# Second-layer MLP: the sums of the first weight's quarters for Strassen's products, moved from GpSimd to DVE

## The chip, the cores and the metric

The kernel runs on one core of one Trainium2 chip, in one launch. The metric is device time in microseconds (us), the median of several runs; the profiled execution is a run of its own with its own time. Engines are called as the profile calls them: PE (TensorE matmul), PEld (its weight load), DVE (VectorE), ACT (ScalarE), POOL (GpSimd), SP (SyncE, which here only issues DMAs).

## What is computed

Two layers of a diffusion backbone over 512 latent tokens, with 256 context tokens that only the first layer carries on. Layer 0 mixes by pooling, layer 1 by grouped-query attention; each ends in an MLP with a squared ReLU. Model width 1024, MLP width 4096, all in float32.

```
def sq_relu_mlp(h, w1, w2):
    return jnp.square(jax.nn.relu(h @ w1)) @ w2
...
    for i in range(DEPTH):
...
        h_lat = h_lat + g1[:, None, :] * y_l
        m_l = modulate(rms_norm(h_lat, norm_g[i, 1]), sh2, sc2)
        h_lat = h_lat + g2[:, None, :] * sq_relu_mlp(m_l, mlp_w1[i], mlp_w2[i])
        if ctx_out:
            h_ctx = h_ctx + cg1[:, None, :] * y_c
            m_c = modulate(rms_norm(h_ctx, norm_g[i, 1]), csh2, csc2)
            h_ctx = h_ctx + cg2[:, None, :] * sq_relu_mlp(m_c, mlp_w1[i], mlp_w2[i])
    return rms_norm(h_lat, final_g)
```

`ctx_out` holds in the first layer only, so the second layer's MLP has the 512 latent tokens alone.

## The kernel before

Every float32 operand of a matmul is split into a high part (float32r, written by ACT, line 86) and a low part (the rest, written by a subtraction on DVE, line 87; `hilo`), and a product is made as high by high, high by low, low by high: three matmuls into one PSUM tile.

`mlp` takes the MLP width in 16 chunks of 256. In chunk c it makes the hidden activations `act` (the first weight, m1), and then the second weight's products of the chunk before (`m2_chunk`, line 490): eight PSUM tiles, each of six matmuls of 512 columns, each added into the residual `h_lat` by one DVE instruction (line 348, called an eviction below). In the second layer chunks 0 to 3 make m1 plainly (line 371; ReLU, two squares on ACT, lines 379 to 382, and the low part on DVE, line 383). Chunks 4 to 15 use Strassen's scheme (`m1_strassen`): seven products of 48 matmuls over halves of both operands in place of eight. For it, each pair of weight tiles is loaded by two DMAs (line 510) into a tile `fin` of two buffers, and five of the seven weight operands are sums or differences of two quarters of it (line 428, into the scratch tile `sc`, 128x512). ACT and DVE then split each operand into high and low parts (lines 433 and 434 for the two that are negated, 86 and 87 for the others). The matmuls (line 439) go to one tile of the PSUM pool `mm` (two buffers) and two of `aux` (four buffers); lines 444 to 450 add the products up, lines 464 to 467 make the activations. The sums on the side of the tokens are made once per layer by DVE (`strassen_inputs`, lines 396, 397 and 87, into `xs`, or in place in `m_m_hi` and `m_m_lo`), beside the first chunks.

At the head of the MLP the normed tokens are made in steps (`modulated`: line 315 on DVE multiplies by the norm, lines 319 on ACT and 321 on DVE scale and shift, then the two parts go to `m_m_hi` and `m_m_lo`); the first chunk's matmuls follow these steps for the second half of the tokens.

Except where an order is written out by hand (the first layer's head), a scheduler of the framework puts each engine's instructions into one queue from priorities, dependences and buffers. Each engine runs its queue strictly in order, so an instruction that waits holds up all that stand behind it. The sums and the low part of the seventh operand were all in POOL's queue, where nothing else stood between them.

`m1_strassen` is used by both layers: the first calls it with `m` set (it needs the context tokens too), the second without.

Of the kernel before, what the change touches and what calls it, by code (L numbers as in the profile page):

```python
# [47 lines left out]
def dit_block_kernel(ctx: ExitStack, tc: tile.TileContext, xT, cols, adab, adaw, w1, w2, wqkv, wo,  # L48
                     poolw, gvec, rope, edge, eye, out):
    nc = tc.nc  # L50
    act, dve, pool, pe = nc.scalar, nc.vector, nc.gpsimd, nc.tensor
# [22 lines left out]
    def new(p, shape, dt, tag, bufs=None):  # L74
        uid[0] += 1
        kw = {"bufs": bufs} if bufs else {}
        return p.tile(shape, dt, tag=tag, name=f"{tag}{uid[0]}", **kw)

    def ps_mm():
        return new(mm, [P, 1024], F32, "mm")  # L80

    def ps_aux():
        return new(aux, [P, 512], F32, "aux")

    def hilo(hi, lo, src, lo_eng=dve):
        act.activation(hi, src, AF.Copy)  # L86
        lo_eng.tensor_tensor(lo, src, hi.bitcast(F32), op=ALU.subtract)  # L87
# [158 lines left out]
    def new_m(name, ctx_too=True):  # L246

        parts = [[big.tile([P, KT, SEQ], F32R, tag=t, name=f"{name}_{t}") for t in ("m_hi", "m_lo")]]
        if ctx_too:
            parts.append([[mc.tile([P, 4, CTX], F32R, tag="mc", name=f"{name}_c{x}{i}") for i in range(2)] for x in range(2)])  # L250
        return parts

    def ms(m, x, k, c0, n):
        if c0 < SEQ:
            return m[0][x][:, k, c0 : c0 + n]
        k0, k = (k.start // 4, slice(k.start % 4, (k.stop - 1) % 4 + 1)) if isinstance(k, slice) else (k // 4, k % 4)
        return m[1][x][k0][:, k, c0 - SEQ : c0 - SEQ + n]
# [153 lines left out]
    def m1_strassen(raw, inputs, a, op, m=None):  # L411


        op = op()
        a11, a12, a21, a22 = (raw[:, i, 512 * j : 512 * j + 512] for i in range(2) for j in range(2))
        ps, px, py = ps_mm(), ps_aux(), ps_aux()
        places = [ps[:, i * 256 : i * 256 + 256] for i in range(4)] + [px[:, :256], px[:, 256:], py[:, :256]]
        parts = [(a11, a12, ALU.add, -1), (a11, None, None, 1), (a22, None, None, 1), (a21, a22, ALU.add, -1),
                 (a12, a22, ALU.subtract, 1), (a21, a11, ALU.subtract, 1), (a11, a22, ALU.add, 1)]
        if m:  # L420
            parts += [(a12, None, None, 1), (a21, None, None, 1)]
        got = []
        for n, (x, y, how, sign) in enumerate(parts):
            w = op(n)
            got.append(w)
            if y is not None:
                t = new(sc, [P, 512], F32, "sc")
                pool.tensor_tensor(t, x, y, op=how)  # L428
                x = t
            if sign > 0:  # L430
                hilo(w[:, 0], w[:, 1], x, pool if n == 6 else dve)
            else:
                act.activation(w[:, 0], x, AF.Copy, scale=-1.0)
                dve.scalar_tensor_tensor(w[:, 1], x, -1.0, w[:, 0].bitcast(F32), op0=ALU.mult, op1=ALU.subtract)
            if n < 7:
                for k in range(4):
                    for wx in range(2):
                        for ax in range(2 - wx):
                            pe.matmul(places[n], w[:, wx, k * P : k * P + P], inputs[n][ax][:, k],  # L439
                                      start=k + wx + ax == 0, stop=k == 3 and wx == 1)  # L440

        q = ps.rearrange("p (q n) -> p q n", q=4)
        t = new(sc, [P, 2, 256], F32, "sc")
        act.activation(t, q[:, 0::3], AF.Copy)
        c, d = (new(rp, [P, T], F32, "r")[:, :512].rearrange("p (q n) -> p q n", q=2) for _ in range(2))
        dve.tensor_tensor(c, q[:, 1:3], t, op=ALU.subtract)
        for i in range(2):
            dve.tensor_tensor(d[:, i], q[:, 2 - i], t[:, i], op=ALU.add)  # L448
        dve.tensor_tensor(d, d, px.rearrange("p (q n) -> p q n", q=2), op=ALU.add)
        dve.tensor_tensor(d, d, py[:, :256].unsqueeze(1).to_broadcast([P, 2, 256]), op=ALU.add)  # L450
        blocks = a.rearrange("p t x (b n) -> p (t x b) n", n=256)
        todo = [(c, c, 1, 5), (d, d, 0, 7)]
        if m:
            pc = ps_aux()
            for t, ws in enumerate(((got[1], got[7]), (got[8], got[2]))):
                for k in range(KT):
                    for wx in range(2):
                        for ax in range(2 - wx):
                            pe.matmul(pc[:, t * 256 : t * 256 + 256], ws[k // 4][:, wx, k % 4 * P : k % 4 * P + P],  # L459
                                      ms(m, ax, k, SEQ, CTX), start=k + wx + ax == 0, stop=k == KT - 1 and wx == 1)  # L460
            todo.append((new(sc, [P, 2, 256], F32, "sc"), pc.rearrange("p (q n) -> p q n", q=2), 2, 6))
        for r, src, o, stride in todo:
            hi, lo = (blocks[:, o + x : o + x + stride + 1 : stride] for x in (0, 3))
            act.activation(r, src, AF.Relu)
            act.activation(hi, r, AF.Square)
            act.activation(r, r, AF.Square)  # L466
            dve.tensor_tensor(lo, r, hi.bitcast(F32), op=ALU.subtract)  # L467
# [29 lines left out]
    def mlp(i, m, total, last, first=None, between=None, ahead=None, strassen=None, acts=(), ws=()):  # L497
        gate = mod[i][:, 40:48]
        prev, acts, sides = None, list(acts), []
        for c in range(NCH):  # L500
# [3 lines left out]
            if not acts:  # L504
                several = 2 if first and c == 0 else 1
                acts = [new(ap_, [P, 2, 2, T], F32R, "act") for _ in range(several)]
                if strassen and c > 1 and c >= strassen[0]:
                    raw = strassen[2]()
                    for t in range(2):
                        nc.sync.dma_start(raw[:, t], w1[i, 2 * c + t])  # L510
                    m1_strassen(raw, inputs, acts[0], strassen[3], m if total > SEQ else None)
                    ws = ()
                else:
                    ws = ws or [load_w(w1[i, 2 * c + t]) for t in range(2 * several)]
                outs = [a[:, t] for a in acts for t in range(2)]
                if not ws:
                    pass
                elif several > 1:
                    m1_chunk(ws, outs, m, first)
                else:  # L520
                    for t in range(2):
                        m1_chunk(ws[t : t + 1], outs[t : t + 1], m, [[(0, total)]])
                ws = ()
# [76 lines left out]
    for s, c0, n in segs:  # L600
        rr = rstd_cols(n, [accs[s]], ps_aux())
        for i in range(n // P):
            t = turned[s][:, i]
# [87 lines left out]
    m = new_m("m")  # L691
# [488 lines left out]
```

## Time and profile before

| what | value |
|---|---|
| median of 3 runs | 1278.03 us (1275.25 to 1279.51) |
| the profiled execution: its own time | 1278.06 us |
| its span, first to last instruction | 1275.9 us (2.2 us lie around it) |
| mean granted clock of PE | 0.993 |
| busy: PE / DVE / ACT / POOL | 1238.5 / 1020.1 / 585.7 / 261.4 us |
| POOL, line 428 on `fin` (second layer) | 60 sums, 96.3 us |
| POOL, line 428 on `pair` (first layer) | 55 sums, 76.6 us |

The span's last 350 us are the second layer's MLP. Times in the timeline are from the span's start. A timeline row gives the start, the time from there to the end of the last of its instructions, engine, line, operation, tiles, and in brackets how long the engine had been idle before it and what ended that. Instructions of one engine overlap a little: the distance between two starts (the pitch) is shorter than the duration of one.

### The profile page before, as it was taken

Reading aid. Unit: us, or ns where it says so; the run is one execution under the profiler, and the core shown is the slowest. Engines: PE = TensorE matmul, PEld = TensorE weight load, DVE = VectorE, ACT = ScalarE, POOL = GpSimd, SP = SyncE. Lnnn points to the kernel's source line nnn. Section 1 sums busy time; section 2 is a strip of 40 time slices with the busy share of each in tenths; the row PEclk is TensorE's granted clock in tenths of the full one; section 3 lists DMA queues with packets and bytes.
Section 4 is the critical chain, followed back from the end, with each engine's and each line's share of the span. In section 5 each row is a group of like instructions: output and inputs, shape, how many; then the busy total and the mean of one; then the engine's idle time right before and its main releaser. Section 6 shows DMA issues by size and latency. Waiting matters only on the chain. (4 is left out here: it accounts for less than half of the span.)

```text
span 1275.9 us, 20565 instructions
## 1 busy us (share of the span) xinstructions
PE 1238.5 (97%) x8150; PEld 1102.5 (86%) x8150; DVE 1020.1 (80%) x1680; ACT 585.7 (46%) x1052; POOL 261.4 (20%) x200
## 2 busy tenths in 40 slices
PE   7999999999999999999999999999989999999997
PEld 6567888899999999999888899899978898989896
DVE  6564998778989888866888378879899889898976
ACT  6445523444444444433455254446554454544443
POOL 0000000122121322231012121211031334343412
PEclk8999999999999999999999999999999999999998
DMA  9666424333433333311113011111223322322111
GB/s 353 263 266 215 135 78 152 116 116 116 148 114 134 118 132 119 118 63 33 56 69 100 20 52 32 65 34 66 100 67 107 125 100 99 100 100 100 67 34 67
DMA packets 41313, 138.68 MB, mean 109 GB/s; under 512 B 4737, under 2 KB 8065, under 8 KB 41089
## 3 DMA queue, kind: packets, MB, share of 16 engines
q1 hardware_dynamic: 41216, 137.36, 30.9%
q8 instruction: 64, 1.05, 0.4%
q14 instruction: 33, 0.26, 0.1%
HBM read 135.25 MB, written 2.10 MB: 108 GB/s over the span
## 5 line engine op out<-in xcount | busy, mean ns | idle before, releaser
L490 PE MATMUL mm<-act,w 128*128 128x512 f32 (+1 forms) x1224 | 237.9, 345 | 3.9 <-DVE act L383 2.1
L490 PE MATMUL aux<-act,w 128*128 128x512 f32 (+1 forms) x1224 | 238.7, 346 | 0.3 <-DVE h_lat L348 0.2
L490 PEld LDWEIGHTS mm<-act,w 128*128 128x128 f32 x1224 | 195.1, 189 | 35.3 <-DVE act L383 2.4
L490 PEld LDWEIGHTS aux<-act,w 128*128 128x128 f32 x1224 | 194.8, 189 | 29.5 <-DVE h_lat L348 0.7
L86 ACT ACTIVATE w<-raw 128x1024 fp32r<-128x1024 f32 x106 | 110.1, 1055 | 124.5 <-PE aux L490 90.0
L428 POOL TENSOR_TENSOR sc<-pair 128x512 f32<-128x512 f32 x55 | 76.6, 1400 | 321.1 <-DVE h_lat L348 107.2
L87 DVE TENSOR_TENSOR w<-raw,w 128x1024 fp32r<-128x1024 f32 x96 | 116.9, 1232 | 28.4 <-ACT w L86 27.9
L348 DVE SCALAR_TENSOR_TENSOR h_lat<-aux,mod,h_lat 128x512 f32<-128x512 f32 (+1 forms) x204 | 125.6, 630 | 16.1 <-PE aux L490 14.7
L428 POOL TENSOR_TENSOR sc<-fin 128x512 f32<-128x512 f32 x60 | 96.3, 1620 | 172.7 <-DVE r L448 83.5
L348 DVE SCALAR_TENSOR_TENSOR h_lat<-mm,mod,h_lat 128x512 f32<-128x512 f32 (+1 forms) x140 | 96.6, 699 | 5.5 <-PE mm L490 4.0
L371 PE MATMUL mm<-m_m_hi,w 128*128 128x512 f32 (+1 forms) x320 | 92.5, 351 | 1.1 <-ACT m_m_hi L86 1.1
L860 PE MATMUL aux<-w,a_m_hi 128*128 128x256 f32 (+1 forms) x384 | 86.3, 320 | 0.0
L219 DVE SCALAR_TENSOR_TENSOR mc<-raw,s_f,mc 128x512 f32<-128x512 f32 x112 | 83.5, 766 | 1.9 <-DMA raw<-in_dram 1.1
L439 PE MATMUL mm<-m_m_hi,mc 128*128 128x256 f32 x384 | 71.0, 283 | 0.0
L860 PEld LDWEIGHTS aux<-w,a_m_hi 128*128 128x128 f32 x384 | 63.4, 190 | 5.0
L371 PEld LDWEIGHTS mm<-m_m_hi,w 128*128 128x128 f32 x320 | 56.1, 189 | 11.0 <-ACT m_m_hi L86 1.3
L459 PE MATMUL aux<-m_c,w 128*128 128x256 f32 x528 | 65.2, 283 | 0.0
L459 PEld LDWEIGHTS aux<-m_c,w 128*128 128x128 f32 x528 | 64.2, 192 | 0.0
L467 DVE TENSOR_TENSOR act<-r,act 128x512 fp32r<-128x512 f32 x46 | 48.4, 1052 | 19.6 <-ACT r L466 19.5
L860 PE MATMUL aux<-w,a_m_lo 128*128 128x256 f32 (+1 forms) x192 | 61.2, 319 | 0.0
L439 PEld LDWEIGHTS mm<-m_m_hi,mc 128*128 128x128 f32 x384 | 60.7, 192 | 0.5
L371 PE MATMUL mm<-m_m_lo,w 128*128 128x512 f32 (+1 forms) x160 | 56.3, 352 | 1.6 <-DVE m_m_lo L87 1.6
(245 smaller groups left out, 2530.5 us busy)
## 6 DMA issues: line engine op xcount, KB each, us to landing
raw<-in_dram SPq DMA_DIRECT2D x157, 512.0 KB, 3.3
praw<-in_dram SPq DMA_DIRECT2D x34, 512.0 KB, 8.2
fin<-in_dram SPq DMA_DIRECT2D x24, 512.0 KB, 4.1
pair<-in_dram SPq DMA_DIRECT2D x22, 512.0 KB, 4.3
block<-in_dram SPq DMA_DIRECT2D x8, 512.0 KB, 6.2
h_lat<-in_dram SPq DMA_DIRECT2D x4, 512.0 KB, 5.9
w<-in_dram SPq DMA_DIRECT2D x4, 512.0 KB, 10.7
out_dram<-fin SPq DMA_DIRECT2D x8, 256.0 KB, 2.5
```

The costliest lines, as they stand in the source:

```text
L86: act.activation(hi, src, AF.Copy)
L87: lo_eng.tensor_tensor(lo, src, hi.bitcast(F32), op=ALU.subtract)
L219: dve.scalar_tensor_tensor(acc[:, s], w, scal, acc[:, s], op0=ALU.mult, op1=ALU.add)
L348: dve.scalar_tensor_tensor(h, ps, gate[:, dt, s : s + 1], h, op0=ALU.mult, op1=ALU.add)
L371: pe.matmul(ps[:, c0 : c0 + cn], lhs, ms(m, ax, k, c0, cn), start=k + wx + ax == 0, stop=k == KT - 1 and wx == 1)
L428: pool.tensor_tensor(t, x, y, op=how)
L439: pe.matmul(places[n], w[:, wx, k * P : k * P + P], inputs[n][ax][:, k], start=k + wx + ax == 0, stop=k == 3 and wx == 1)
L459: pe.matmul(pc[:, t * 256 : t * 256 + 256], ws[k // 4][:, wx, k % 4 * P : k % 4 * P + P], ms(m, ax, k, SEQ, CTX), start=k + wx + ax == 0, ...
L467: dve.tensor_tensor(lo, r, hi.bitcast(F32), op=ALU.subtract)
L490: pe.matmul(ps, lhs, a[:, t, ax, c0 : c0 + n], start=t + wx + ax == 0, stop=t == 1 and wx == 1)
L860: pe.matmul(ps, lhs, ws[u][:, wx, o : o + width], start=k + ax + wx == 0, stop=k == KT - 1 and ax == 1)
```

## The change

In the second layer the engine of the five sums, and of the low part of the seventh operand, becomes DVE; in the first layer both stay on POOL.

```
     def m1_strassen(raw, inputs, a, op, m=None):
-        op = op()
+        op, eng = op(), pool if m else dve
...
             if y is not None:
                 t = new(sc, [P, 512], F32, "sc")
-                pool.tensor_tensor(t, x, y, op=how)
+                eng.tensor_tensor(t, x, y, op=how)
                 x = t
             if sign > 0:
-                hilo(w[:, 0], w[:, 1], x, pool if n == 6 else dve)
+                hilo(w[:, 0], w[:, 1], x, eng if n == 6 else dve)
```

So 60 sums and 12 subtractions, 72 instructions of 128x512, leave POOL's queue and stand in DVE's. The queues of PE and ACT change only in order, from the head of the second layer's MLP on; the DMA queue has one load moved by one place. Three places of DVE's queue follow, each as the difference (+ is the changed kernel).

First the head of the MLP, last quarter of the normed tokens (`sc_9629` is its scratch tile, `sc_9623` that of the quarter before; `fin_10284` is the first weight pair for Strassen; `mc_9894` and `mc_9895` are token sums):

```order
 L315 TENSOR_TENSOR sc_9629<-h_lat,mc_9609 128x512
+L428 TENSOR_TENSOR sc_10292<-fin_10284 128x512
+L87 TENSOR_TENSOR m_m_lo<-sc_9623,m_m_hi 128x2x256
 L321 TENSOR_SCALAR sc_9629<-sc_9629,am_140,mod_135 128x256
-L87 TENSOR_TENSOR m_m_lo<-sc_9623,m_m_hi 128x2x256
+L428 TENSOR_TENSOR sc_10339<-fin_10284 128x512
+L428 TENSOR_TENSOR sc_10356<-fin_10284 128x512
 L87 TENSOR_TENSOR m_m_lo<-sc_9629,m_m_hi 128x2x256
 L396 TENSOR_TENSOR mc_9894<-m_m_hi 128x1024
+L428 TENSOR_TENSOR sc_10372<-fin_10284 128x512
 L396 TENSOR_TENSOR mc_9895<-m_m_lo 128x1024
 L87 TENSOR_TENSOR w_9884<-raw_9885,w_9884 128x1024
```

Three sums now stand ahead of the last quarter's low part, and a fourth between the two token sums behind it.

Then the rows right behind these, up to the low part of the first activations (`act_9645`, line 383), which the first m2 block needs:

```order
 L87 TENSOR_TENSOR h_ctx_10287<-sc_10372,h_ctx_10287 128x512
 L397 TENSOR_TENSOR mc_9894<-mc_9894,mc_9895 128x1024
-L396 TENSOR_TENSOR mc_10046<-m_m_hi 128x1024
-L396 TENSOR_TENSOR mc_10047<-m_m_lo 128x1024
+L428 TENSOR_TENSOR sc_10388<-fin_10284 128x512
 L383 TENSOR_TENSOR act_9645<-r_9861,act_9645 128x512
 L383 TENSOR_TENSOR act_9645<-r_9866,act_9645 128x512
```

Two token sums of 1024 columns went behind the activations, and the fifth weight sum came ahead of them.

Last a chunk in the run of equal ones (`sc_11833`, `sc_11850`, `sc_11866` are sums for the next chunk; `mm_11703` and the like are m2 tiles being evicted):

```order
 L348 SCALAR_TENSOR_TENSOR h_lat<-mm_11703,mod_135,h_lat 128x512
-L434 SCALAR_TENSOR_TENSOR mc_11832<-sc_11833,mc_11832 128x512
+L428 TENSOR_TENSOR sc_11833<-fin_11778 128x512
 L348 SCALAR_TENSOR_TENSOR h_lat<-mm_11711,mod_135,h_lat 128x512
 L467 TENSOR_TENSOR act_11565<-r_11689,act_11565 128x2x256
 L348 SCALAR_TENSOR_TENSOR h_lat<-aux_11719,mod_135,h_lat 128x512
+L434 SCALAR_TENSOR_TENSOR mc_11832<-sc_11833,mc_11832 128x512
+L428 TENSOR_TENSOR sc_11850<-fin_11778 128x512
+L348 SCALAR_TENSOR_TENSOR h_lat<-aux_11727,mod_135,h_lat 128x512
+L428 TENSOR_TENSOR sc_11866<-fin_11778 128x512
+L348 SCALAR_TENSOR_TENSOR h_lat<-mm_11735,mod_135,h_lat 128x512
```

Sums and evictions now alternate, with at most two other instructions between two evictions, and at least two rows between a sum and the instruction that splits it.

## Rows read from the trace of the kernel before

**Rows 1.** Stretches: length, busy time of engines (instructions), PE's clock, DMA share, GB/s.
```profile
925.00:945.00 20.00, 15.25 (x119) 14.32 (x118) 19.12 (x20) 11.27 (x19) 8.53 (x5) 1.00 0.08 27
945.00:966.50 21.50, 21.50 (x94) 17.37 (x94) 21.15 (x24) 11.37 (x16) 1.99 (x1) 1.00 0.41 128
...
1009.92:1030.90 20.98, 20.98 (x133) 19.08 (x133) 18.01 (x25) 9.82 (x18) 8.84 (x7) 1.00 0.29 102
...
1177.76:1198.74 20.98, 20.98 (x133) 19.09 (x133) 18.01 (x25) 9.82 (x18) 8.85 (x7) 1.00 0.29 101
```

**Rows 2.** Timeline of PE at the head of the second layer's MLP.
```profile
930.02 0.50 PE L371 MATMUL mm<-m_m_hi,w 128*128 128x256 f32 x2 [1.05 <-ACT m_m_hi L86]
...
932.02 0.39 PE L371 MATMUL mm<-m_m_lo,w 128*128 128x256 f32 x1 [0.79 <-DVE m_m_lo L87]
...
933.93 0.39 PE L371 MATMUL mm<-m_m_lo,w 128*128 128x256 f32 x1 [0.81 <-DVE m_m_lo L87]
...
942.31 0.39 PE L490 MATMUL mm<-act,w 128*128 128x512 f32 x1
944.80 1.20 PE L490 MATMUL mm<-act,w 128*128 128x512 f32 x4 [2.10 <-DVE act L383]
```

**Rows 3.** Chain that ended last, in order of time: start, length, what.
```profile
956.15 10.88 PE mm L371 x48
...
1020.83 5.75 PE mm L439 x48
```

**Rows 4.** Timeline of DVE at the head of the second layer's MLP.
```profile
927.86 1.38 DVE L321 TENSOR_SCALAR sc<-sc,am,mod 128x256 f32<-128x256 f32 x1
929.16 1.75 DVE L315 TENSOR_TENSOR sc<-h_lat,mc 128x512 f32<-128x512 f32 x1
930.96 0.41 DVE L321 TENSOR_SCALAR sc<-sc,am,mod 128x256 f32<-128x256 f32 x1
...
932.25 1.63 DVE L87 TENSOR_TENSOR m_m_lo<-sc,m_m_hi 128x512 fp32r<-128x512 f32 x1 [0.28 <-ACT m_m_hi L86]
...
934.93 2.31 DVE L396 TENSOR_TENSOR mc<-m_m_lo 128x1024 f32<-128x1024 f32 x1
...
940.69 2.32 DVE L396 TENSOR_TENSOR mc<-m_m_hi 128x1024 f32<-128x1024 f32 x1
...
944.07 1.28 DVE L383 TENSOR_TENSOR act<-r,act 128x512 fp32r<-128x512 f32 x2
```

**Rows 5.** The same stretch, POOL and ACT.
```profile
927.48 2.89 POOL L428 TENSOR_TENSOR sc<-fin 128x512 f32<-128x512 f32 x2 [4.59 <-issue]
...
936.20 0.63 ACT L86 ACTIVATE h_ctx<-sc 128x512 fp32r<-128x512 f32 x1 [3.98 <-POOL sc L428]
...
939.72 1.15 ACT L382 ACTIVATE r<-r 128x512 f32<-128x512 f32 x2
```

**Rows 6.** Timeline of DVE in chunks of Strassen products.
```profile
1008.19 1.79 DVE L87 TENSOR_TENSOR mc<-fin,mc 128x512 fp32r<-128x512 f32 x1
...
1010.51 1.19 DVE L87 TENSOR_TENSOR mc<-fin,mc 128x512 fp32r<-128x512 f32 x1
...
1012.22 1.52 DVE L467 TENSOR_TENSOR act<-r,act 128x512 fp32r<-128x512 f32 x1
...
1015.58 1.33 DVE L467 TENSOR_TENSOR act<-r,act 128x512 fp32r<-128x512 f32 x1
...
1017.49 0.68 DVE L87 TENSOR_TENSOR mc<-sc,mc 128x512 fp32r<-128x512 f32 x1
...
1019.35 1.40 DVE L348 SCALAR_TENSOR_TENSOR h_lat<-mm,mod,h_lat 128x512 f32<-128x512 f32 x2
...
1042.97 2.35 DVE L87 TENSOR_TENSOR w<-raw,w 128x1024 fp32r<-128x1024 f32 x2
1048.29 0.69 DVE L446 TENSOR_TENSOR r<-mm,sc 128x512 f32<-128x512 f32 x1 [2.97 <-ACT sc L444]
```

**Rows 7.** One tile, `fin`: its loads, durations of the issue, first and last start.
```profile
L510 SPq DMA_DIRECT2D fin<-in_dram x24: 327/422/502, 908.5 to 1180.0; - x24
```

## The prediction, made before the changed kernel ran

> **What bounds the kernel now.** I read the stretches first, then PE's timeline where a stretch shows PE idle, then DVE's and POOL's at the same place. In the chunks of Strassen products PE is busy for all of each 20.98 us period; nine such periods follow each other, the first and the last of them shown, and DVE is busy for 18.01 us of each, POOL for some 8.8 [rows 1]. PE is the bound there, and neither a quicker POOL nor a slower one is felt. The reader should then see the one stretch of the second layer's MLP ahead of its tail where PE is not full: at its head, 925 to 945, PE is busy 15.25 us of 20 and DVE 19.12 [rows 1]. PE's timeline names the four waits: 1.05, 0.79 and 0.81 us for the parts of the normed tokens, then 2.10 for the low part of the first activations (line 383) [rows 2]. All hang on DVE, directly or through ACT. And DVE is not only busy there, it is held up. Instructions that take 0.41 and 0.68 us elsewhere take 1.38, 1.75 and 1.63 us, and two token sums of 1024 columns take 2.31 and 2.32 [rows 4], where two others of that size take 2.35 together [rows 6]. POOL's sums run at those moments [rows 5]. So the removal of POOL's work has two sides: DVE gets 72 instructions more, and loses what POOL's reads cost it.
>
> **The cost of one instruction.** No sum of line 428 has run on DVE in the second layer. The nearest rows are its other 128x512 instructions with two operands in SBUF: 0.68 us long, and 0.60 from start to start when they follow each other (1.28 for two, less 0.68) [rows 4, 6]. Lower bound 0.60, upper bound 1.79, the longest of that shape beside POOL [rows 6]. I take 0.60, since POOL will be empty and the queue full. [...]
>
> **Equal chunks.** A chunk adds 6 x 0.60 = 3.60 us to DVE. It gives back the stretching: two low parts of line 87 (1.79 and 1.19 against 0.68) and two of line 467 (1.52 and 1.33 against 0.68) [rows 6], 1.11 + 0.51 + 0.84 + 0.65 = 3.11. So 18.01 + 3.60 - 3.11 = 18.50 us of 20.98; DVE's idle 2.97 ahead of line 446 [rows 6] shrinks to about 2.5. The cover is this idle time, and PE does not wait if no single step is late. An eviction is due every 6 x 0.227 = 1.36 us (48 matmuls of 512 columns in 10.88 [rows 3]); an eviction (0.70 at most [rows 6]) and one other instruction fit into that. Only between the third and the fourth do two stand: 0.70 + 2 x 0.60 = 1.90, some 0.5 late, while a PSUM tile is wanted again only two or more tiles, 2.7 us, later. Each sum stands two or more rows ahead of the low part that needs ACT's 0.63 us in between [rows 5]. The weight tile `fin` has two buffers and arrives a chunk early, so the first sum does not wait for its DMA. Eleven periods change by 0. If the cover were gone, each 0.1 us over would cost 1.1 us in all.
>
> **The head, first wait group.** Walk DVE from 927.86, at plain pitch: line 321 to 928.2, line 315 to 928.8, the first sum to 929.4, the third quarter's low part written by 930.1, line 321, two sums, and the last quarter's low part from 931.5 to 932.2, against 932.25 + 1.63 = 933.88 before [rows 4]: the three sums (1.8 us) cost less than the stretching (0.97 + 1.07 + 0.95 = 3.0) and DVE's idle 0.28. The weights have long landed (issue at 908.5 [rows 7]). ACT's high part of the third quarter is there at 928.8, just as PE comes to it (it stopped at 930.02 - 1.05 = 928.97 [rows 2]). PE then has 26 matmuls of 256 columns, at 5.75/48 = 0.12 us [rows 3], up to the last quarter's low part, so reaches it at about 932.2, and 58 more end at 939.2. Before, the first m2 matmul started at 942.31 [rows 2]. **Gain 3.1 us.**
>
> **The head, second wait.** DVE's next: token sum, weight sum, token sum, weight part, operand part, token sum (line 397), weight sum: 4 x 1.14 + 3 x 0.60 = 6.4, so 932.2 to 938.6; then line 383. Before it stood behind two more token sums and began at 944.07 [rows 4]. ACT held the same chain up: it sat idle 3.98 us for a POOL sum until 936.20, and came to line 382 at 939.72 [rows 5]. After, the ReLU needs PE's 29 matmuls behind 932.2, so starts at 935.9, and six steps of ACT at half of 1.15 or less [rows 5] end with line 382 at 938.6 and 939.1; line 383 is done at 939.3 and 939.9. PE arrives at 939.2 and its second matmul needs the first of these: a wait of 0.1 in place of 944.80 - 942.31 - 0.23 = 2.26 [rows 2]. **Gain 2.2.**
>
> **The rest of the first m2 block.** From 944.80 it lasted to 956.15 [rows 2, 3]: 11.35 us for 47 matmuls that need 47 x 0.227 = 10.66, 0.69 lost where a PSUM tile waited for the second activations' ReLU. That dependence stays; by the same walk ACT clears the tile at 941.2, PE would want it at 941.0. **Gain 0.5**, and the block ends at 939.2 + 0.1 + 10.9 + 0.2 = 950.4, 5.75 us early.
>
> **From there to the equal chunks.** PE was full between 945 and 1009.92, but DVE too: 21.15 of 21.50 [rows 1]. PE is 5.75 us ahead, DVE less: the five stretched instructions (3.0, and 2 x 1.13 for the token sums) and the idle 0.28 are 5.5, less six instructions of 0.60: 1.9 [rows 4]. The other 3.8 come out of DVE's lead over PE. Walking on in its order, the closest place is the low part of the next weight tile: done at 949, PE wants it at 950.4. The token sum for the third product is done at 994.9, wanted at 996.9. No wait, 0. The queue moves are: SP one load, POOL emptied to the four last multiplications, whose order stays.
>
> Sum: 3.1 + 2.2 + 0.5 = 5.8, or 5.75 by the end of the block. The profiled execution took 1278.06, against a median of 1278.03: the two are the same within 0.03. **1278.06 - 5.75 = 1272.3.**
>
> **Rivals.**
>
> *DVE decides in the fill stretch.* If the lead is smaller than walked, PE falls back to what DVE gains: 1.9 us, 1276.2. For it: 21.15 of 21.50 busy [rows 1]. Against: the closest margin walked is 1.4 us.
>
> *DVE becomes the bound of the equal chunks (slower).* The stretching would not be POOL's doing, but stay. Then DVE needs 18.01 + 3.60 = 21.61 of 20.98 per chunk, 0.63 x 11 = 6.9 us; at the head six instructions (3.6) come in and only the idle 0.28 goes out, 3.3 more: 1278.06 + 10.2 = 1288.3. It decides once less than 0.63 us of the 3.11 goes away. Against: the same form takes 0.68 when POOL is idle and 1.79 beside it [rows 6]. [...]
>
> *Nothing is felt.* The head's gain is lost to a wait that I do not see further on: 1278.
>
> **How the numbers follow.** Forecast 0.72, DVE in the fill stretch 0.17, DVE the bound 0.07, nothing felt 0.04. A measurement tells 0.3%, 3.8 us, from no change, so faster means below 1274.2. The second and fourth case lie within; with a little of the forecast's own spread over the line: faster 0.72, same 0.20, slower 0.08. Range: below, all 3.1 + 2.26 + 0.69 = 6.05 comes back (1272.0) and the median lies up to 2.8 under, as the lowest run of before did: 1269.2. Above, the fill-stretch rival and the 1.5 that the highest run of before lay over the median: 1277.7. The slower rival stays outside.
>
> **What would show it.** Right: POOL idle from about 923 to the tail; DVE's line 87 and 467 at 0.68 throughout; L428 on DVE at 0.68; nine or more periods of 20.98; PE's waits at the head below 0.3 us in sum, the first m2 block ending near 950.4, the first Strassen chunk near 994 in place of 999.85. Wrong: periods above 21.0 with PE waiting for lines 348 or 87 (DVE the bound); idle PE between 950 and 1005 (fill stretch); line 383 still the last to come at the head.

## The result, and the profile after

The changed kernel took 1271.11 us in the median of six runs (1269.62 to 1272.20), the kernel before 1277.82 beside it: a ratio of 0.9949, 95% interval 0.9938 to 0.9959, so 5.2 to 7.9 us less. The profiled execution took 1270.80 us, with a span of 1268.8 (before 1278.06 and 1275.9).

Stretches of the second layer's MLP (columns as in [rows 1]): its head, the stretch behind it, and the place of the first equal chunk shown there.

```profile
925.00:945.00 20.00, 19.93 (x137) 18.10 (x137) 19.83 (x28) 14.25 (x24) 0.00 (x0) 1.00 0.17 53
945.00:966.50 21.50, 21.50 (x96) 17.84 (x95) 21.12 (x25) 9.31 (x12) 0.00 (x0) 1.00 0.44 146
...
1002.83:1023.81 20.98, 20.98 (x134) 19.09 (x133) 18.74 (x30) 10.15 (x16) 0.00 (x0) 1.00 0.28 101
```

Before, PE was busy 15.25 us of the first stretch; now 19.93. The periods are the same 20.98: line 446 of an equal chunk starts at 1020.22 and, nine chunks on, at 1209.04.

PE's timeline at the place of [rows 2]: the first m2 matmuls, the first matmul behind the first m2 block, and the first product of line 439. None of the rows between has idle time in brackets.

```profile
938.01 0.88 PE L490 MATMUL mm<-act,w 128*128 128x512 f32 x3
...
938.95 0.67 PE L490 MATMUL mm<-act,w 128*128 128x512 f32 x2
...
949.08 0.39 PE L371 MATMUL mm<-m_m_hi,w 128*128 128x512 f32 x1
...
992.60 0.28 PE L439 MATMUL mm<-m_m_hi,mc 128*128 128x256 f32 x1
```

DVE's timeline at the place of [rows 4], from line 315's first start on, with the sums now in it:

```profile
922.79 1.29 DVE L315 TENSOR_TENSOR sc<-h_lat,mc 128x512 f32<-128x512 f32 x2 [1.99 <-ACT mc L304]
...
926.55 0.41 DVE L321 TENSOR_SCALAR sc<-sc,am,mod 128x256 f32<-128x256 f32 x1
926.88 0.68 DVE L315 TENSOR_TENSOR sc<-h_lat,mc 128x512 f32<-128x512 f32 x1
927.48 0.68 DVE L428 TENSOR_TENSOR sc<-fin 128x512 f32<-128x512 f32 x1
928.08 0.69 DVE L87 TENSOR_TENSOR m_m_lo<-sc,m_m_hi 128x512 fp32r<-128x512 f32 x1
...
930.21 0.68 DVE L87 TENSOR_TENSOR m_m_lo<-sc,m_m_hi 128x512 fp32r<-128x512 f32 x1
930.81 1.22 DVE L396 TENSOR_TENSOR mc<-m_m_hi 128x1024 f32<-128x1024 f32 x1
...
937.40 1.29 DVE L383 TENSOR_TENSOR act<-r,act 128x512 fp32r<-128x512 f32 x2 [0.16 <-ACT r L382]
```

What took 1.38, 1.75, 1.63 and 2.31 us takes 0.41, 0.68, 0.68 and 1.22, and from line 315's first start DVE comes to line 383 after 14.6 us (922.79 to 937.40) in place of 20.0 (924.11 to 944.07), though five sums stand ahead of it now, for two token sums that moved behind.

In the equal chunks, groups of instructions by line and shape (count, busy us, mean ns, idle before them) over nine of them, 1003.5 to 1192; before:

```profile
L87 DVE TENSOR_TENSOR mc<-fin,mc 128x512 fp32r<-128x512 f32 x18 | 26.9, 1494 | 0.0
L467 DVE TENSOR_TENSOR act<-r,act 128x512 fp32r<-128x512 f32 x18 | 25.7, 1426 | 0.0
```

and after:

```profile
L428 DVE TENSOR_TENSOR sc<-fin 128x512 f32<-128x512 f32 x45 | 30.6, 681 | 0.0
L87 DVE TENSOR_TENSOR mc<-fin,mc 128x512 fp32r<-128x512 f32 x18 | 12.3, 683 | 0.0
L467 DVE TENSOR_TENSOR act<-r,act 128x512 fp32r<-128x512 f32 x18 | 12.3, 682 | 0.0
L446 DVE TENSOR_TENSOR r<-mm,sc 128x512 f32<-128x512 f32 x9 | 6.2, 691 | 19.1 <-ACT sc L444 19.1
```

(26.9 - 12.3 + 25.7 - 12.3) / 9 = 3.11 us a chunk come back from the stretching; DVE's idle time ahead of line 446 falls from about 3.0 us to 2.12 (19.1 / 9) in each.

One measure serves for all runs below, since the stretch ahead of the head varies by some us from run to run: the time from line 315's first start to the first product of line 439 in this layer, called **the head's length**. The two rows before, of DVE and PE:

```profile
924.11 1.29 DVE L315 TENSOR_TENSOR sc<-h_lat,mc 128x512 f32<-128x512 f32 x2 [1.99 <-ACT mc L304]
...
999.68 0.28 PE L439 MATMUL mm<-m_m_hi,mc 128*128 128x256 f32 x1
```

Before: 924.11 to 999.68, 75.57 us. After: 922.79 to 992.60, 69.81. So the head gives 5.76; from there to the end the two traces keep the same distance within 0.1 us. The span differs by 7.2, of which 1.3 lies ahead of the head, where the queues are the same.

### The profile page after: what moved, and what is told of

The parts are those of the page before. It is cut to its first block, busy times and chain, and to the rows that moved or that the text cites. A ratio compares the mean times of both kernels' runs of the same rounds, so it can differ in the third digit from the quotient of the medians.

```text
span 1268.8 us, 20479 instructions
## 1 busy us (share of the span) xinstructions
PE 1236.7 (97%) x8150; PEld 1103.4 (87%) x8150; DVE 1026.2 (81%) x1752; ACT 588.7 (46%) x1052; POOL 149.1 (12%) x128
## 4 chain that ended last, share of the span: by engine, by line
PE 62%; issue 27%; DVE 7%; ACT 2%; POOL 1%; DMA 1%; SPq 0%; POOLq 0%; DVEq 0%; ACTq 0%
PE mm L490 10%; PE aux L490 10%; PE aux L860 6%; PE mm L371 6%; PE aux L459 5%; PE mm L439 5%; PE aux L439 4%; PE aux L986 3%; PE aux L187 2%; PE mm L645 2%; PE mm L732 1%; PE aux L974 1%; PE aux L961 1%; PE mm L938 1%; PE mm L621 1%
## 5 line engine op out<-in xcount | busy, mean ns | idle before, releaser
L286 POOL TENSOR_TENSOR sm<-sm,neghalf 128x2 f32<-128x2 f32 (+1 forms) x11 | 8.9, 811 | 509.9 <-DVE sm L284 509.9
L439 PE MATMUL mm<-m_m_lo,mc 128*128 128x256 f32 x192 | 54.4, 283 | 0.0
```

## Experiments

The theory: GpSimd's reads of SBUF hold DVE up, at the head that is on PE's path, in the equal chunks it is not. The rivals: the gain comes from elsewhere than the head; or from the sums' place in the queues, not from the stretching.

**1 and 2. Where the gain lies.** Two complementary halves of the change:

```
-        op, eng = op(), pool if m else dve
+        op, eng = op(), dve if not m and c == 4 else pool     # 1
+        op, eng = op(), pool if m or c == 4 else dve          # 2
```

> DVE makes the sums in the first Strassen chunk of the second layer's MLP alone (c = 4); in its eleven other Strassen chunks GpSimd makes them as before. Theory (everything comes from the head, where GpSimd's reads hold DVE up): the whole gain, 1271 to 1272 us, PE without waits at the head, the first m2 block's end near 949 as in the changed kernel, periods of 20.98 us; lines 87 and 467 stretched again to above 1.1 us in the equal chunks. Rival (a part of the gain comes from the eleven other chunks or from the tail): less than the whole, 1274 or above.

> The complement: GpSimd makes the sums in the chunk c = 4 as before, DVE those in the eleven others. Theory: nothing is gained, 1277 to 1278 us, PE's waits at the head as before (some 5 us in sum), periods of 20.98 us with DVE idle 2.1 us in each. Rival (a part of the gain comes from the other chunks or from the tail): the remainder of what the first kernel lacks, 1275 or below.

The first took 1270.52 us (ratio 0.9942, 0.9929 to 0.9956), head's length 69.84; the second 1278.05 (1.0002, 0.9992 to 1.0013), 75.59. Their stretches 1030 to 1051; the first kernel,

```profile
1030.00:1051.00 21.00, 21.00 (x133) 19.09 (x132) 18.04 (x24) 9.85 (x17) 8.85 (x6) 1.00 0.31 101
```

and the second:

```profile
1030.00:1051.00 21.00, 21.00 (x134) 19.11 (x133) 18.79 (x30) 10.16 (x16) 0.00 (x0) 1.00 0.27 101
```

The second's waits of PE at the head are those of the kernel before: 2.1 us for line 383, 1.6 for two low parts of the normed tokens, 1.0 for a high part.

All of the gain is in the one chunk whose sums fall into the head. In the eleven others DVE is busy 0.75 us more, and PE full either way.

**3. GpSimd keeps the sums, but later.** On the kernel before, ahead of the first sum of chunk 4:

```
-                pool.tensor_tensor(t, x, y, op=how)
+                n or m or c != 4 or pool.tensor_scalar(t[:, :4], inputs[4][0][:, 0, :4].bitcast(F32), 0.0, None, op0=ALU.mult); pool.tensor_tensor(t, x, y, op=how)
```

> The kernel before, with GpSimd making every sum, but its sums for the chunk c = 4 wait for the high part of the third product's token operand (about 949 us): a four-column GpSimd instruction that reads that part and writes into the tile of the first sum stands ahead of them; the sum overwrites it. Theory (GpSimd's reads beside DVE's instructions cost the time at the head, and the sums' own place is indifferent): DVE's lines 315, 321, 87 and 396 at the head take 0.4 to 1.2 us in place of 1.4 to 2.3, PE's waits there fall from 4.75 us to below 1, the first m2 block ends at 949 to 951; what GpSimd then takes from DVE lies behind 949, where PE has a lead: 1272 to 1275 us in all. Rival (the gain comes from the sums being ready sooner on DVE, and ACT no longer waiting for them in its queue ahead of line 382): the first wait group stays, 1276 us or above. If GpSimd's late sums hold DVE up in the full stretch 950 to 1005, PE waits there, and the time lies between 1275 and 1280.

1276.09 us (0.9983, 0.9974 to 0.9992): above the theory's 1272 to 1275, inside the range named for late sums that hold DVE up. At the head the theory holds: from line 315 to the end of the first m2 block it takes 26.36 us, against 31.87 before and 26.29 in the changed kernel, with not one sum on DVE. DVE comes to line 383 13.5 us after line 315 (924.67 to 938.19), with the two token sums still ahead of it: their move was not needed for the gain. Then most of it is lost again. Stretches of this run:

```profile
925.00:945.00 20.00, 19.93 (x144) 18.52 (x143) 19.68 (x27) 15.28 (x25) 0.57 (x2) 1.00 0.23 76
945.00:966.50 21.50, 18.93 (x84) 15.32 (x83) 20.58 (x20) 9.30 (x13) 8.67 (x6) 0.99 0.31 102
966.50:984.00 17.50, 17.50 (x72) 14.35 (x71) 15.56 (x20) 5.67 (x9) 0.54 (x1) 0.91 0.25 85
```

and the rows of its timeline, of ACT, DVE and PE:

```profile
950.92 0.63 ACT L86 ACTIVATE h_ctx<-sc 128x512 fp32r<-128x512 f32 x1 [4.68 <-POOL sc L428]
...
954.66 2.31 DVE L87 TENSOR_TENSOR xs<-mc,xs 128x1024 fp32r<-128x1024 f32 x1
...
964.41 1.06 ACT L86 ACTIVATE xs<-mc 128x1024 fp32r<-128x1024 f32 x1 [4.14 <-DVE mc L397]
...
966.01 2.75 PE L490 MATMUL mm<-act,w 128*128 128x512 f32 x6 [2.57 <-ACT r L379]
```

GpSimd's sums now run beside DVE's low parts behind 945 (2.31 us in place of 1.22), ACT waits for GpSimd and then for a late token sum of DVE, and PE for ACT: 2.57 us, and some 1.6 more at a granted clock of 0.91 behind that. The edit moved ACT's copies of the sums behind line 382 too, so this run alone does not part stretching from queue order; run 9 does.

**4. GpSimd reads beside the equal chunks again.** The changed kernel, with useless sums on GpSimd:

```
                 eng.tensor_tensor(t, x, y, op=how)
+                m or c < 6 or pool.tensor_tensor(idle[0], x, y, op=how)
```

> The changed kernel, plus GpSimd making the five sums of each chunk once more, into a tile that nothing reads, in the last ten Strassen chunks of the second layer (c > 5). Theory (GpSimd's reads stretch DVE's instructions that have all operands in SBUF, and in the changed kernel DVE has 2.1 us to spare per chunk): lines 87, 428 and 467 are stretched again, to 1.0 to 1.8 us; DVE needs 18.8 us and 2.5 to 4 more of a period of 20.98, so the periods grow by 0 to 0.8 us and the time lies at 1271 to 1279 us. Rival (the stretching was not GpSimd's doing but came from the place of those instructions in the queue): lines 87, 428 and 467 stay at 0.68 us, periods of 20.98 us, 1271 us.

1270.98 us (0.9947, 0.9933 to 0.9961): no loss. But the stretching is back. Groups over eight chunks, 1020 to 1190:

```profile
L428 POOL TENSOR_TENSOR idle<-fin 128x512 f32<-128x512 f32 x42 | 69.6, 1656 | 120.0 <-DMA fin<-in_dram 117.6
L87 DVE TENSOR_TENSOR mc<-fin,mc 128x512 fp32r<-128x512 f32 x17 | 24.4, 1436 | 0.0
```

and the row of DVE's timeline that has idle time ahead of it in the changed kernel:

```profile
1061.33 0.68 DVE L446 TENSOR_TENSOR r<-mm,sc 128x512 f32<-128x512 f32 x1
```

Line 446 has no idle time ahead of it any more, but for 0.25 us in one of the eight: the stretching ate the 2.1 us that DVE had to spare, and the periods stayed at 20.98. It is GpSimd's doing, and with that much to spare it cost nothing here.

**5 and 6. What a sum costs there, and the bound.** The changed kernel with three (5) or all (6) of the sums made twice:

```
-                eng.tensor_tensor(t, x, y, op=how)
+                for _ in range(2 if not m and c > 4 and n in (0, 3, 4) else 1): eng.tensor_tensor(t, x, y, op=how)     # 5
+                for _ in range(2 if not m and c > 4 and True else 1): eng.tensor_tensor(t, x, y, op=how)     # 6
```

> The changed kernel, in whose last eleven Strassen chunks (c > 4) DVE makes three of the five sums twice, into the same tile, with the same result. Theory (a sum costs DVE 0.60 us and it has 2.1 us to spare in a period of 20.98): 3 x 0.60 = 1.8 us more, DVE's idle ahead of line 446 falls to about 0.3 us, periods of 20.98 us, 1271 to 1272 us. Rival (a sum costs more than its 0.60 us, or single steps come late before the queue is full): periods above 21.1 us, 1273 us or more.

> The same with all five sums made twice. Theory: 5 x 0.60 = 3.0 us more against 2.1 us to spare, so each of eleven periods grows by some 0.9 us to 21.9, DVE has no idle time left and PE waits for it: 1271 + 10 = 1281 us (1278 to 1284). Rival (DVE's idle time is not its true reserve, because PE's waits would not follow from a full queue): 1273 us or below.

Run 5: 1271.15 us (0.9940, 0.9923 to 0.9957), periods of 20.98, DVE busy 20.8 of 21.0. Run 6: 1284.9 us (1.0052, 1.0033 to 1.0071), over the expected range. Line 446 in DVE's timeline of run 6, eight chunks apart:

```profile
1041.66 0.69 DVE L446 TENSOR_TENSOR r<-mm,sc 128x512 f32<-128x512 f32 x1
...
1218.84 0.69 DVE L446 TENSOR_TENSOR r<-mm,sc 128x512 f32<-128x512 f32 x1
```

(1218.84 - 1041.66) / 8 = 22.15 us a period, 1.17 over, where 0.9 was expected; PE now waits at the chunks' first products for ACT's line 433 (6.2 us in five waits), which waits for a sum. A sum costs more than 0.60 here: from 18.01 to 18.77 busy with 3.11 given back, the six added instructions cost (0.76 + 3.11) / 6 = 0.65 each, and 18.77 + 5 x 0.65 = 22.0. With DVE's queue full, the period grew by what this sum gives, 22.0 - 20.98 = 1.02 us, and by 0.15 more.

**7. More work for DVE behind the head.** As run 6, for `c == 4` alone.

> The changed kernel, in whose first Strassen chunk alone (c = 4) DVE makes the five sums twice, with the same result. In DVE's queue no more sums stand ahead of the last low part of the normed tokens than in the changed kernel; three of the five added ones stand between it and line 383, for which a copy's low part and a line 397 now stand behind line 383; the rest lies behind. DVE's work in the stretch 930 to 995 grows by 3.0 us. Theory (PE's lead holds in the full stretch because DVE has a reserve of 1.4 us at its closest place there): PE stays without waits to line 383, and waits 1 to 2 us in all further on: 1272 to 1273.5 us. Rival A (the reserve is larger than 3 us): 1271 us. Rival B (DVE has no reserve in that stretch): all of 3.0 us, 1274 us.

1272.44 us (0.9949, 0.9929 to 0.9969), head's length 69.84, and 0.2 us more in the chunk behind it. The time lies in the theory's range, but PE has none of the waits that the theory named; by the trace it is rival A but for 0.2. The scheduler put token sums further back for it, so that the closest places got nothing of the 3.0 us; DVE still had its idle time of the equal chunks to catch up in.

**8. The first layer too.** `op, eng = op(), dve`.

> The changed kernel with the sums on DVE in the first layer's MLP too, so that GpSimd makes none. Theory (where PE is full neither a quicker nor a slower GpSimd is felt; in the first layer PE is busy for all of 410 us of its eleven chunks while DVE is busy 23 to 31 of some 33.5 us in each): no difference to the changed kernel beyond 1 us, 1270 to 1272 us, lines 87 and 467 of the first layer at 0.68 us. Rival A (PE's order there is made with POOL's sums in view, and the chain of waits names them twice, 1.69 us each): 2 to 4 us faster, 1267 to 1269 us. Rival B (DVE, busy 30.7 of 33 to 36 us in four of the chunks, becomes late): slower, 1273 us or more.

1272.19 us (0.9951, 0.9937 to 0.9965), 0.2 above the range named and not told from the changed kernel. The first layer's chunks, 215 to 625, in the changed kernel,

```profile
215.00:625.00 410.00, 409.84 (x2823) 378.19 (x2822) 330.64 (x532) 172.56 (x276) 88.53 (x65) 1.00 0.32 109
```

and here:

```profile
215.00:625.00 410.00, 409.67 (x2825) 378.11 (x2824) 355.57 (x599) 175.50 (x274) 0.70 (x1) 1.00 0.32 109
```

PE is full both times. That the chain of waits names a GpSimd sum there did not make it one that decides.

**9. Reads alone, at the head.** The changed kernel, its queues of PE, DVE and ACT in the same order, with GpSimd reading behind each of the five sums of chunk 4:

```
                 eng.tensor_tensor(t, x, y, op=how)
+                m or c != 4 or pool.tensor_tensor(idle[0], t, y, op=how)
```

> The changed kernel, plus one GpSimd instruction of 128x512 behind each of DVE's five sums of the first Strassen chunk (c = 4): it adds the sum and a quarter of the weight into a tile that nothing reads. PE, DVE and ACT keep their order; ACT waits for none of it. Theory (at the head it is GpSimd's reads of SBUF that hold DVE up): DVE's lines 87, 396, 321 and 428 there are stretched by 0.5 to 1.2 us each again, PE waits at the head 1 to 4 us, 1272 to 1275 us. Rival (the gain at the head came from the sums' place, and from ACT no longer waiting for GpSimd ahead of line 382): DVE's instructions stay at 0.41, 0.68 and 1.22 us, PE full, 1271 us.

1277.15 us (0.9988, 0.9978 to 0.9999), above the range of 1272 to 1275: the kernel before took 1278.19 beside it, so 1.0 of some 6.7 us of gain is left. The head's length is 74.90, 5.09 over the changed kernel's. POOL's timeline,

```profile
932.00 1.62 POOL L428 TENSOR_TENSOR idle<-sc,fin 128x512 f32<-128x512 f32 x1 [6.72 <-DVE sc L428]
934.50 3.30 POOL L428 TENSOR_TENSOR idle<-sc,fin 128x512 f32<-128x512 f32 x2 [0.88 <-POOL idle L428]
939.63 2.14 POOL L428 TENSOR_TENSOR idle<-sc,fin 128x512 f32<-128x512 f32 x1 [1.83 <-DVE sc L428]
945.26 1.68 POOL L428 TENSOR_TENSOR idle<-sc,fin 128x512 f32<-128x512 f32 x1 [3.50 <-DVE sc L428]
```

DVE's:

```profile
932.38 1.38 DVE L321 TENSOR_SCALAR sc<-sc,am,mod 128x256 f32<-128x256 f32 x1
...
934.89 1.77 DVE L87 TENSOR_TENSOR m_m_lo<-sc,m_m_hi 128x512 fp32r<-128x512 f32 x1
936.58 2.30 DVE L396 TENSOR_TENSOR mc<-m_m_hi 128x1024 f32<-128x1024 f32 x1
...
940.54 2.30 DVE L87 TENSOR_TENSOR w<-raw,w 128x1024 fp32r<-128x1024 f32 x1
...
945.11 2.38 DVE L383 TENSOR_TENSOR act<-r,act 128x512 fp32r<-128x512 f32 x2
```

and two rows of PE:

```profile
945.84 0.73 PE L490 MATMUL mm<-act,w 128*128 128x512 f32 x2 [0.20 <-DVE act L383]
...
947.54 0.50 PE L490 MATMUL mm<-act,w 128*128 128x512 f32 x1 [0.51 <-DVE act L383]
```

Five reading instructions of GpSimd, five instructions of DVE stretched, by 0.97, 1.09, 1.08, 1.08 and 1.10 us; every other at its plain duration. ACT waits for none of this, and the sums stand where the changed kernel has them. DVE, without idle time on the way, is done with line 383 at 21.0 us after line 315's first start (926.50 to 947.49), against 15.9 in the changed kernel (922.79 to 938.69) and 21.2 before (924.11 to 945.35). So the reads alone take back 5.1 of the 5.3 us, and the rival, that the gain came from the queue order, falls. PE's waits are 0.81 and 0.84 us for the normed tokens and 0.20 and 0.51 for line 383; between 935 and 940 it ran at a granted clock of 0.72 (last section).

Four of the five stretched instructions have two SBUF tensors. The fifth, line 321 (1.38 us in place of 0.41), has one tensor and two scalars; how a read of GpSimd holds up an instruction of DVE, no run here shows.

**10 and 11. Writes.** In place of run 9's addition, in run 10 a read of four columns and two writes of the unread tile; in run 11 the read behind the first sum alone, and four writes behind each.

```
+                m or c != 4 or (pool.tensor_scalar(idle[0][:, :4], t[:, :4], 0.0, None, op0=ALU.mult), pool.memset(idle[0], 0.0), pool.memset(idle[0], 0.0))     # 10
+                m or c != 4 or ([pool.tensor_scalar(idle[0][:, :4], t[:, :4], 0.0, None, op0=ALU.mult)] if n == 0 else []) + [pool.memset(idle[0], 0.0) for _ in range(4)]     # 11
```

> The same, but at each of the five places GpSimd does a four-column instruction that reads the sum, and then sets the unread tile of 128x512 to zero twice: it is busy about as long, writes SBUF, and reads all but nothing of it. Theory (reads against reads): DVE is not stretched, 1270.5 to 1272 us, the same as the changed kernel. Rival (any work of GpSimd on SBUF holds DVE up, its writes too): DVE's instructions stretched as beside the reading ones, 1272 to 1275 us.

> The run with the writing GpSimd again, without what held it up there: of the four-column reads only the first is left, so that no sum's tile waits for GpSimd to be free again; behind it GpSimd sets the unread tile of 128x512 to zero twenty times in a row, some 12 us, over the whole head. Theory (reads against reads; the time lost in the run before came from its small reads, the longest of which took 6.50 us and kept a sum's tile, for which DVE waited 3.08 us): DVE's instructions at 0.41, 0.68 and 1.22 us, no wait of DVE for GpSimd, PE full, 1270.5 to 1272 us. Rival (GpSimd's writes cost DVE or PE time in another way): PE waits at the head again, 1273 us or more.

Run 10: 1274.77 us (0.9966, 0.9952 to 0.9979), outside of the theory's range, though no instruction of DVE is stretched. Rows of POOL, DVE and PE say why:

```profile
932.10 6.50 POOL L428 TENSOR_SCALAR idle<-sc 128x4 f32<-128x4 f32 x1
...
941.60 0.69 DVE L428 TENSOR_TENSOR sc<-fin 128x512 f32<-128x512 f32 x1 [3.08 <-POOL idle L428]
...
942.95 1.22 PE L490 MATMUL mm<-act,w 128*128 128x512 f32 x2 [2.68 <-DVE act L383]
```

The second of the small reads lasted 6.50 us, to 938.60, for as long as DVE's instructions on SBUF followed each other without a gap. So the later ones came late, and DVE's fifth sum, which needed a scratch tile that the fourth of them (941.34 to 941.57) still had to read, stood 3.08 us, with line 383 behind it in DVE's queue, and PE stood 2.68 us for that line. The held read began that wait; the two pairs of writes that stood ahead of the fourth read in GpSimd's queue, 1.11 us each (from 938.67 and 940.15), made up most of its length. So this run does not part the two, and run 11 leaves out the later reads. Head's length 74.09, 4.28 over the changed kernel's.

Run 11: 1271.14 us (0.9945, 0.9931 to 0.9959), head's length 69.81, as the changed kernel. POOL's row, and the stretch:

```profile
932.23 11.75 POOL L428 MEMSET idle<- 128x512 f32 x20
```

```profile
925.00:945.00 20.00, 19.93 (x148) 18.68 (x149) 18.72 (x27) 13.44 (x24) 11.18 (x21) 1.00 0.09 27
```

GpSimd is busier at the head than before the change (11.18 against 8.53 us), and nothing is stretched: it is its reads that count, not its being at work.

No version measured is told from the changed kernel to the better side; the best median, 1270.52 of run 1, lies inside its interval.

## Why the prediction was right

1272.3 was forecast and 1271.11 measured, within the range and on the side that had 0.72. Step by step:

- **One sum on DVE.** 0.60 from start to start at the head (927.48 to 928.08), as taken; 0.65 in the equal chunks. The bound of 1.79 was far off.
- **Equal chunks.** The 3.11 us given back came out to the last digit (the groups above). The added 3.60 was mis-sized: 3.87. So DVE needs 18.77, not 18.50, and has 2.1 us left, not 2.5. It costs nothing: periods of 20.98, run 2 shows no change, run 5 that the reserve is real, run 6 where it ends. The single steps walked there (evictions between sums) held: PE has no wait.
- **The head, first wait group.** From line 315 to the first m2 matmul: 942.31 - 924.11 = 18.20 before [rows 2], 938.01 - 922.79 = 15.22 after: 2.98, against 3.1. The last low part was ready 7.42 + 0.68 us after line 315 (930.21 - 922.79), with no wait of PE.
- **The head, second wait.** The second m2 matmul follows the first without a gap: all 2.26 came back, against 2.2 with a wait of 0.1 left. ACT was what came last, as walked, but by 0.16 us of DVE's time and none of PE's.
- **The rest of the first m2 block.** From the first m2 matmul to the first matmul behind the block: 955.98 - 942.31 = 13.67 before, 949.08 - 938.01 = 11.07 after, 2.60 less. Without the second wait, 2.60 - 2.26 = 0.34, against 0.5. The block's end comes 5.58 us early, not 5.75.
- **From there to the equal chunks.** No wait, as said, against the rival that had 0.17. From the block's end to line 439 it is 43.70 us before and 43.52 after: 0.18 more comes back, where 0 was named. The next weight tile's low part was done at 946.54 + 1.22 = 947.76, wanted at 949.08: 1.3 us to spare against a walked 1.4. The first product of line 439 starts at 992.60, where 994 was named; the 1.3 us between lie ahead of the head. Run 3 shows how real that rival was: with GpSimd's reads moved there, 4.3 of the 5.5 us were lost again (head's length 74.38).
- **Rival "DVE becomes the bound".** Its condition, that stretching stays without GpSimd, is refuted by runs 9 and 11 from one side and run 4 from the other: lines 87 and 396, each with two SBUF tensors, took 1.77 and 2.30 us beside run 9's reads, 0.68 and 1.22 in the changed kernel and in run 11. The rows set against it, 0.68 us with POOL idle and 1.79 beside it [rows 6], were right.
- **The size.** 5.75 was forecast, 5.76 is in the traces, and the medians differ by 6.7. That 5.75 and 5.76 agree to 0.01 us is luck: the four terms came out as 2.98, 2.26, 0.34 and 0.18 for 3.1, 2.2, 0.5 and 0, and their errors cancel. What lies between 5.76 and 6.7 was not in the prediction, though the interval (5.2 to 7.9) takes in 5.76. The granted clock goes some way: in the 60 executions of the kernel before that the runs were compared with, PE's mean granted clock was 0.9917, in the 27 of the changed kernel and of runs 1, 4, 5 and 11, which have its head without a wait, 0.9934. At equal clock the two differ less:

| mean clock | before, mean us (executions) | changed head, mean us (executions) | difference |
|---|---|---|---|
| 0.990 | 1280.04 (16) | none | |
| 0.991 | 1278.22 (13) | 1272.72 (2) | 5.5 |
| 0.992 | 1277.58 (11) | 1272.34 (6) | 5.2 |
| 0.993 | 1277.34 (15) | 1271.06 (4) | 6.3 |
| 0.994 | 1276.12 (5) | 1271.11 (8) | 5.0 |
| 0.995 | none | 1269.58 (7) | |

So some 5.5 us are the waits themselves, and the rest goes with a clock that is lower, on the mean, where PE waits at the head. That the waits are what lowers it is argued from this and from the rows below; the one traced execution of before had 1.00 there, so it is not shown for that kernel.

## What to carry to other kernels

Price a GpSimd instruction by what its reads take from VectorE, not by GpSimd's own time: at this head each sum of 128x512 cost VectorE 0.95 to 1.10 us by being run beside it, and 0.60 by being run on it (0.65 in the equal chunks). In the equal chunks six GpSimd instructions held up four of VectorE's, by 3.11 us together. Whether that was felt depended here on the place alone (1270.52 us in run 1, 1278.05 in run 2): count what VectorE has to spare in the stretch where the tensor engine waits for it, and where a period has some microseconds to spare, leave things as they are. Moving GpSimd's reads to a later time instead only pays if they land where VectorE has that room: run 3 lost 4.3 of 5.5 us again.

## What the runs showed that I had not expected

A GpSimd read was held up too: four columns took 6.50 us in run 10, while seven VectorE instructions followed each other, where the next two took 0.23 each. So a small GpSimd read of a tile that is used again can start a wait, there one of 3.08 us of VectorE. When a read is let in stays open: those of run 9 did get in between VectorE's instructions.

A wait of PE was in three runs followed by a lower granted clock. Run 10, stretches of 5 us at the head (columns as in [rows 1]):

```profile
940.00:945.00 5.00, 2.32 (x7) 1.67 (x6) 3.40 (x5) 2.71 (x5) 4.23 (x9) 0.77 0.00 0
945.00:950.00 5.00, 5.00 (x21) 4.03 (x20) 5.00 (x7) 4.42 (x7) 0.00 (x0) 0.89 0.32 108
```

After the wait of 2.68 us, up to 942.95, the granted clock is 0.77 and then 0.89, each over 5 us; PE's timeline there:

```profile
943.97 0.63 PE L490 MATMUL aux<-act,w 128*128 128x512 f32 x1
944.40 1.05 PE L490 MATMUL mm<-act,w 128*128 128x512 f32 x2
```

A matmul of 512 columns takes 0.43 us (943.97 to 944.40) where 0.227 is usual [rows 3]. The head's length is 4.28 us over the changed kernel's, of which 2.68 are the wait, so some 1.6 go with the clock. Run 3 lost 1.6 us in the same way behind its 2.57. In run 9 the clock fell as well behind two waits of 0.81 and 0.84 us:

```profile
935.00:940.00 5.00, 4.16 (x25) 3.95 (x24) 5.00 (x4) 1.54 (x2) 3.09 (x3) 0.72 0.00 0
```

Up to line 383 that cost nothing: DVE came to that line without idle time of its own, and PE had to wait for it even so. The kernel before waited as long at its head with a clock of 1.00 [rows 1], so a lower clock does not follow every wait.
